# Down projections of a two-layer decoder trunk: two kinds of weight differences and one pair of activation differences take a later place in VectorE's order

## The chip, the cores and the metric

The kernel runs on one core of a Trainium2 chip. The metric is the device time of one execution in microseconds (us). The engines are named as in the profile: PE is TensorE, PEld its weight loads, DVE is VectorE, ACT is ScalarE, POOL is GpSimd, and SP is the engine that issues most DMAs, in the order of its queue.

## What is computed

The reference is a decoder trunk of two layers over 1024 tokens of width 1024, in float32. Each layer has a mixer (retention and RWKV heads in layer 0, sliding-window attention in layer 1), and after it a dense feed-forward block. The change touches only the last product of that block, the down projection with 2816 inputs:

```python
def swiglu(h, w_gate, w_up, w_down):
    return (jax.nn.silu(h @ w_gate) * (h @ w_up)) @ w_down
...
    h = h + swiglu(n, ffn_w_gate[layer], ffn_w_up[layer], ffn_w_down[layer])
```

## The kernel before

**Precision.** Every float32 operand of a product is split in two: a high part (a cast on ACT to fp32r) and a low part (a subtraction of the cast from the source, on POOL or DVE). A product is three matmuls, high by high, high by low, low by high: lines 1182, 1183 and 1184 of `prod`. For a weight tile `vsplit` makes the cast on ACT (line 1370) and the low part on POOL (line 1371). The split weights go through six buffers in turn (`w` and `wr`), so a cast waits until PE has finished with the weight six places earlier. For an activation tile `split` makes the cast on ACT (line 356) and the low part on POOL or DVE (line 358).

**The down projection.** `down` (line 1400) multiplies 2 by 2 blocks with seven products instead of eight, after Strassen and Winograd. The 2816 inputs come in 22 tiles of 128, that is 11 pairs p (NP = 11); tokens come in two halves of 512 (h0 and h1); outputs come in eight tiles, that is four pairs dp. `DGROUPS` cuts the pairs p into groups: (0, 4) and (4, 8) in layer 0, whose rest goes another way, and (0, 4), (4, 8) and (8, 11) in layer 1. In a group of n pairs each of the four dp has a raw weight block of four parts, a11, a12, a21 and a22, from the buffers `wd0` (a11, a12) and `wd1` (a21, a22). DVE forms from them, always at line 1397 because all go through the helper `vop`:

- S1 = a21 + a22 (a buffer `ws`), and S2 = S1 - a11 (a second buffer `ws`), both in the first round;
- the third difference, S3 = a11 - a21, written over a21 in `wd1` (called at line 1446);
- the fourth difference, S4 = a12 - S2, written over S2 in its `ws` buffer (called at line 1451), so that it must wait until ACT and POOL have read S2.

**Rounds.** A group is seven rounds on PE. In each round the four dp have an accumulator (PSUM bank) of their own, and each takes 3n matmuls of 128x128 by 128x512. The weights of the rounds are: 1 a11, 2 S2, 3 a12, 4 S3, 5 a22, 6 S1, 7 S4. The activations are tiles of the hidden product or of its sums and differences: round 1 and 3 plain tiles of half 0, round 7 plain tiles of half 1 (loaded into `hr`, then split; the SP line is 1381), and round 2, 4, 5 and 6 differences that were split earlier, written to the DRAM array `hc`, and are loaded again by `sums8` (SP, line 1376) into buffers `n8` and `ha`. Behind each accumulator DVE adds the result into h0 or h1; in round 1 ACT copies it to a buffer u0 (line 1434).

**Where the differences of the activations come from.** `form_down` (line 1313) makes four differences for a pair p: a subtraction on DVE (line 1318), a split, and a DMA to `hc` from SP (line 1325). For all pairs but the last it runs during the feed-forward loop before. For the last pair of layer 1 (p = 10) it is handed to `down` as `rest` and is traced there between rounds 4 and 5 of the first group (line 1460). For that pair the low part of the split is on DVE, and the two tiles that hold a split serve in turn, so the third one waits for the first DMA. Its results are first needed in the last group.

**Order of the work.** The kernel is traced in program order, and a scheduler then orders each engine's instructions, by when it takes their inputs to be ready. `behind` adds an ordering edge between two instructions of one engine without a wait on a semaphore; `keep` pins an instruction behind all that was traced on its engine before. The loads and stores of `down` on SP are kept in this way, in program order: on SP the four stores of pair 10 (line 1325) stand ahead of the four loads of round 6 (line 1376, tiles `ha`), these ahead of the raw tiles of round 7 (line 1381), and these ahead of the next group's weights and tiles.

In the order before, DVE takes S3 of a dp right behind that dp's S2 where it is free, and S4 wherever it is ready. It runs the four subtractions of pair 10 (line 1318) ahead of the first S1 of layer 1's first group, and their low parts (line 358) in round 4.

Of the kernel before, what the change touches and what calls it, by code (L numbers as in the profile page):

```python
# [13 lines left out]
ALU = mybir.AluOpType  # L14
# [9 lines left out]
NP = FT // 2  # L24
# [180 lines left out]
class Kern:  # L205
# [456 lines left out]
    def pair(self, u, hf, p):  # L662
# [123 lines left out]
        for w in range(2):  # L786
# [4 lines left out]
            mean = self.t(mp, [P, 32], "vm", 2)[:, :8].rearrange("p (a b) -> p a b", b=2)  # L791
            V.tensor_reduce(out=mean, in_=ps, axis=AX.X, op=ALU.add, negate=True)

# [33 lines left out]
    def unit(self, u, hf, pairs):  # L827
# [10 lines left out]
        for q in range(2):  # L838
            nc.sync.dma_start(DT[64 * q : 64 * q + 64], dn)
        X = self.t(mp, [P, 16, 32], "X", 1)  # L840
        Xf = X.rearrange("p a b -> p (a b)")
        G.memset(Xf, 0.0)
# [4 lines left out]
        for j in range(31):  # L847
            n, m = j // 2 + 1, 31 - j
            tv = tmp[:, : n * m].rearrange("p (a b) -> p a b", b=m)
            V.tensor_tensor(  # L850
                out=tv, in0=X[:, 0:n, j : j + 1].to_broadcast([P, n, m]),
                in1=DT[:, j : j + 1, j + 1 : 32].to_broadcast([P, n, m]), op=ALU.mult,
            )
            V.tensor_tensor(out=X[:, 0:n, j + 1 : 32], in0=X[:, 0:n, j + 1 : 32], in1=tv, op=ALU.add)
            if j % 2:
                yield (), 1.9
        for q in range(2):
            nc.sync.dma_start(dg.rearrange("u (i q) t -> q u i t", q=2)[q], X[64 * q : 64 * q + 64])
        if u:
# [453 lines left out]
    def form_down(self, L, p, x, ts):  # L1313

        nc = self.nc

        def put(i, o, a, b):
            nc.vector.tensor_tensor(out=o, in0=a, in1=b, op=ALU.subtract)
            t = ts[i in (2, 3)]
            self.split(o, t[:, 0, :], t[:, 1, :], p < NP - 1)  # L1320
            d = (self.hc[L][p, i - 1], t.bitcast(F32))
            if p == NP - 2 and i > 2:
                self.owed.append(d)
            else:
                (nc.gpsimd if p == NP - 2 else nc.sync).dma_start(*d)
            return o

        tmp = lambda: self.t(self.pp, [P, HT], "nq", 4)
        yield
        t1 = put(1, x["11"], x["12"], x["11"])  # L1330
        yield
        t2 = put(2, tmp(), x["22"], t1)
        yield
        put(4, tmp(), x["21"], t2)
        yield
        put(3, tmp(), x["22"], x["12"])
        yield
# [62 lines left out]
    def down(self, L, fp, fz, rest, X, first):  # L1400


        op, S = self.vop, self.nc.scalar
        h0, h1 = (self.kt(self.h[hf]) for hf in range(2))
        dps = range(KT // 2)
        j, ends = len(X), []

        def place():
            nonlocal j
            i, j = j % (12 if L else 14), j + 1  # L1410
            if i >= 8 if L else i < 6:
                return self.t(fp, [P, 2, HT], "ha", 4 if L else 6, F32R)
            return self.t(self.pp, [P, 2, HT], "n8", 8, F32R)

        def plain(hf, f):
            return self.plain8(L, hf, f, place(), self.t(fp, [P, HT], "hr", 4))

        for gi, g in enumerate(DGROUPS[L]):
            n, ps = g[1] - g[0], range(*g)
            ta, tb = ("fffy", "mmrc")[:: 1 - 2 * (gi % 2)]  # L1420
            s1, u0, a1 = [], [], []
            W = [self.wdown(L, 0, g, fp, "wd0", 5)]
            X = X or [plain(0, 2 * p) for p in ps]
            W += [self.wdown(L, 2 * i, g, fp, "wd0", 5) for i in (1, 2, 3)]
            for i in dps:
                W[i] += self.wdown(L, 2 * i + 1, g, fp, "wd1", 6 - L)
            A = [self.pst(t, [P, HT]) for t in ta]
            first += [self.vsplit(W[dp][0]) for dp in dps[len(first) :]]
            cast = self.last_cast
            for dp in dps:  # L1430
                a11, a12, a21, a22 = W[dp]
                self.prod(A[dp], first[dp], X, True, False)
                u0.append(self.t(fz, [P, HT], "u0", 4))
                self.behind(S.copy(u0[dp], A[dp]), cast)
                s1.append(op(self.wsum(fp, n, 4, 8), a21, a22))
                if ends:
                    self.behind(self.last_vop, ends[dp])
                a1.append(a11)
                W[dp][0] = op(self.wsum(fp, n, 4, 8), s1[dp], a11, ALU.subtract)
            X = [self.sums8(L, p, 2, place()) for p in ps]  # L1440
            B = [self.pst(t, [P, HT]) for t in tb]
            for dp in dps:
                self.prod(B[dp], self.vsplit(W[dp][0]), X, True, False)
                y = op(self.t(fz, [P, HT], "y", 2), B[dp], u0[dp])
                op(h1(2 * dp), h1(2 * dp), y)
                op(W[dp][2], a1[dp], W[dp][2], ALU.subtract)
            X = [plain(0, 2 * p + 1) for p in ps]
            for dp in dps:
                self.prod(A[dp], self.vsplit(W[dp][1]), X, False, True)
                op(h0(2 * dp), h0(2 * dp), A[dp])  # L1450
                op(W[dp][0], W[dp][1], W[dp][0], ALU.subtract)
            X = [self.sums8(L, p, 3, place()) for p in ps]
            for dp in dps:
                self.prod(B[dp], self.vsplit(W[dp][2]), X, False, False)
                y = op(self.t(fz, [P, HT], "y", 2), B[dp], u0[dp])
                op(h1(2 * dp + 1), h1(2 * dp + 1), y)
            X = [self.sums8(L, p, 4, place()) for p in ps]
            while self.owed:
                self.keep(self.nc.sync.dma_start(*self.owed.pop(0)))
            for _ in rest:  # L1460
                pass
            for dp in dps:
                self.prod(B[dp], self.vsplit(W[dp][3]), X, False, True)
                op(u0[dp], B[dp], u0[dp])
                op(h0(2 * dp + 1), h0(2 * dp + 1), u0[dp])
            X = [self.sums8(L, p, 1, place()) for p in ps]
            X6 = [plain(1, 2 * p + 1) for p in ps]
            if g[1] == NP:
                yield
            A = [self.pst(t, [P, HT]) for t in ta]  # L1470
            for dp in dps:
                self.prod(A[dp], self.vsplit(s1[dp]), X, True, False)
                op(h1(2 * dp + 1), h1(2 * dp + 1), A[dp])
            ends, first = [], []
            for dp in dps:
                self.prod(A[dp], self.vsplit(W[dp][0]), X6, False, True)
                op(h1(2 * dp), h1(2 * dp), A[dp])
                ends.append(self.last_vop)
            X = ()
        yield  # L1480
# [402 lines left out]
```

## Time and profile before

| what | value |
|---|---|
| median of 3 runs | 2357.8 us (2355.4 to 2360.68) |
| the profiled execution's own time | 2357.52 us |
| its span in the profile | 2355.7 us |
| mean granted clock of PE | 0.993 of full speed |
| first group of layer 0, round 2 begins | 1156.50 us after the start of the span |
| first group of layer 1, round 2 begins | 2137.63 us after the start of the span |

Times in the rows are microseconds from the start of the span, and a second number is the duration, which is given in nanoseconds only where the profile says so. A row of the timeline has start, duration, engine, line, operation, output<-input, shapes and how many instructions were merged, and in square brackets how long the engine had been idle and what ended that. A row of the waits has the waiting engine, tile and line, behind the arrow the releaser, then the sum in us, how many waits, and the longest. Matmuls overlap, so what one costs is read from the distance of the starts. The span leaves out about 1.8 us of the execution's own time.

### The profile page before, as it was taken

The page shows a single profiled execution, that of the slowest core. Times are in us where ns is not written, and L with a number is a line of the kernel's source. Part 1 is how long each engine was busy: PE and PEld are TensorE (multiplying, and loading weights), DVE is VectorE, ACT ScalarE, POOL GpSimd, SP SyncE. Part 2 cuts the span into 40 slices and gives each one's busy share as a digit, 9 for nine tenths or more (in the row PEclk, how much of TensorE's full clock was granted, in tenths as well). Part 3 has the DMA queues.
Part 4 walks back from the last instruction along what each step waited for, and adds up shares of the span by engine and source line. Part 5 has one row for each costly group of instructions (what it writes and reads, how often), then busy time and mean ns, then how long its engine had stood idle before and what let it go on. Part 6 is the DMA issues. An engine that isn't in the chain of part 4 may idle for free.

```text
span 2355.7 us, 35610 instructions
## 1 busy us (share of the span) xinstructions
PE 2306.3 (98%) x13092; PEld 1826.9 (78%) x13092; DVE 1650.4 (70%) x2628; ACT 1051.2 (45%) x1944; POOL 953.7 (40%) x748
## 2 busy tenths in 40 slices
PE   8999999999999999999999999999999999999998
PEld 6777677777777888888888877677788888887886
DVE  6876865765657448887676568667647788888766
ACT  5354433323556333333333556556635333333335
POOL 3123221201342057777577300002201677776776
PEclk9999999999999999999999999999999999999999
DMA  7655543433445646554574321131236466656663
GB/s 275 211 192 199 172 152 130 127 123 117 143 165 171 209 161 212 213 204 172 181 267 146 128 79 57 67 132 71 95 117 216 172 219 216 216 201 245 257 213 114
DMA packets 168317, 398.02 MB, mean 169 GB/s; under 512 B 42960, under 2 KB 45648, under 8 KB 168144
## 3 DMA queue, kind: packets, MB, share of 16 engines
q1 hardware_dynamic: 165024, 390.24, 47.6%
q10 hardware_dynamic: 2832, 4.45, 0.5%
q8 instruction: 104, 1.70, 0.3%
q0 software_dynamic: 288, 1.05, 0.1%
q14 instruction: 69, 0.57, 0.1%
HBM read 273.39 MB, written 116.92 MB: 166 GB/s over the span
## 4 chain that ended last, share of the span: by engine, by line
PE 75%; DVE 10%; DMA 5%; issue 4%; ACT 3%; POOL 1%; SPq 1%; DVEq 0%; ACTq 0%; POOLq 0%
PE ps_m L1182 7%; PE ps_m L1184 7%; PE ps_m L1183 7%; PE ps_f L240 6%; PE ps_f L352 5%; PE ps_f L351 5%; PE ps_f L350 5%; PE ps_m L240 4%; PE ps_f L1182 4%; PE ps_f L1184 4%; PE ps_f L1183 4%; PE ps_r L1182 2%; PE ps_r L1184 2%; PE ps_r L1183 2%; PE ps_c L1182 2%
## 5 line engine op out<-in xcount | busy, mean ns | idle before, releaser
L240 PE MATMUL ps_f<-n,w 128*128 128x512 f32 x1440 | 386.5, 416 | 10.8 <-ACT w L335 6.3
L240 PEld LDWEIGHTS ps_f<-n,w 128*128 128x128 f32 x1440 | 269.4, 193 | 95.4 <-issue 24.1
L335 ACT CAST w<-wr 128x512 fp32r<-128x512 f32 x244 | 148.0, 612 | 184.2 <-PE ps_f L352 71.3
L336 POOL TENSOR_TENSOR w<-wr,w 128x512 fp32r<-128x512 f32 x68 | 91.5, 1354 | 280.5 <-ACT w L335 223.4
L336 DVE TENSOR_TENSOR w<-wr,w 128x512 fp32r<-128x512 f32 (+1 forms) x176 | 123.4, 704 | 73.7 <-ACT w L335 73.5
L336 POOL TENSOR_TENSOR w<-wq,w 128x512 fp32r<-128x512 f32 x92 | 131.2, 1438 | 39.3 <-ACT w L335 36.9
L350 PE MATMUL ps_f<-n,w 128*128 128x512 f32 x356 | 141.4, 397 | 0.7 <-ACT n L1629 0.5
L351 PE MATMUL ps_f<-n,w 128*128 128x512 f32 x356 | 141.7, 398 | 0.0
L352 PE MATMUL ps_f<-n,w 128*128 128x512 f32 x356 | 140.9, 396 | 0.6 <-POOL w L336 0.6
L336 POOL TENSOR_TENSOR wx<-wr,wx 128x512 fp32r<-128x512 f32 x8 | 10.5, 1318 | 303.1 <-ACT wx L335 302.9
L1191 DVE TENSOR_TENSOR nq<-ps_m,u 128x512 f32<-128x512 f32 x88 | 58.9, 684 | 99.3 <-PE ps_m L1184 99.1
L1182 PE MATMUL ps_f<-n,w 128*128 128x512 f32 x298 | 117.4, 395 | 1.6 <-ACT u L1342 1.6
L1182 PE MATMUL ps_m<-n,w 128*128 128x512 f32 x300 | 117.6, 392 | 0.0
L1184 PE MATMUL ps_m<-n,w 128*128 128x512 f32 x300 | 116.9, 390 | 0.0
L1183 PE MATMUL ps_m<-n,w 128*128 128x512 f32 x300 | 116.8, 389 | 0.0
L1183 PE MATMUL ps_f<-n,w 128*128 128x512 f32 x298 | 116.1, 390 | 0.0
L1184 PE MATMUL ps_f<-n,w 128*128 128x512 f32 x298 | 115.9, 391 | 0.0
L1182 PE MATMUL ps_m<-cb,w 128*128 128x512 f32 x240 | 93.6, 390 | 1.3 <-DVE nq L1191 1.3
L1184 PE MATMUL ps_m<-cb,w 128*128 128x512 f32 x240 | 93.4, 389 | 0.0
L1183 PE MATMUL ps_m<-cb,w 128*128 128x512 f32 x240 | 93.4, 389 | 0.0
L358 POOL TENSOR_TENSOR n<-nq,n 128x512 fp32r<-128x512 f32 x54 | 91.6, 1708 | 4.0 <-ACT n L356 4.0
L1371 POOL TENSOR_TENSOR w<-wd,w 128x512 fp32r<-128x512 f32 (+1 forms) x51 | 72.3, 1427 | 36.9 <-ACT w L1370 36.9
(532 smaller groups left out, 6447.1 us busy)
## 6 DMA issues: line engine op xcount, KB each, us to landing
hc<-n SPq DMA_DIRECT2D x74, 512.0 KB, 2.7
wsp<-w SPq DMA_DIRECT2D x54, 512.0 KB, 3.7
w<-wsp SPq DMA_DIRECT2D x54, 512.0 KB, 3.4
wq<-in_w_gate SPq DMA_DIRECT2D x44, 512.0 KB, 4.2
u<-u SPq DMA_DIRECT2D x88, 256.0 KB, 3.0
n<-hc SPq DMA_DIRECT2D x43, 512.0 KB, 5.9
wr<-in_w_in SPq DMA_DIRECT2D x34, 512.0 KB, 5.1
hid<-n SPq DMA_DIRECT2D x66, 256.0 KB, 2.0
```

Source lines behind the costliest of these rows:

```text
L240: self.nc.tensor.matmul(out, lhsT, rhs, **kw)
L335: nc.scalar.copy(hi[:, :n], raw[:, c])
L336: self.lo.tensor_tensor(out=lo[:, :n], in0=raw[:, c], in1=hi.bitcast(F32)[:, :n], op=ALU.subtract)
L350: nc.tensor.matmul(ps, hi, rh, start=k == 0, stop=False)
L351: nc.tensor.matmul(ps, hi, rl, start=False, stop=False)
L352: nc.tensor.matmul(ps, lo, rh, start=False, stop=k == n - 1)
L358: e.tensor_tensor(out=lo, in0=src, in1=hi.bitcast(F32), op=ALU.subtract)
L1182: mm(ps, hi, xh, start=first and k == 0, stop=False, skip_group_check=True)
L1183: mm(ps, hi, xl, start=False, stop=False, skip_group_check=True)
L1184: mm(ps, lo, xh, start=False, stop=last and k == len(w) - 1, skip_group_check=True)
L1191: self.last_add = V.tensor_tensor(out=o, in0=x, in1=y, op=ALU.add)
L1371: nc.gpsimd.tensor_tensor(out=lo, in0=v, in1=hi.bitcast(F32), op=ALU.subtract)
```

## The change

S3 and S4 of every dp get an ordering edge behind the last S2 of their group (`s2`). The subtractions of pair 10 in layer 1 are kept behind all DVE work that was traced before them, which ends with the additions of round 4 of the first group. No instruction is added or removed, and SP's order is the same in both kernels.

```diff
@@ form_down
         def put(i, o, a, b):
-            nc.vector.tensor_tensor(out=o, in0=a, in1=b, op=ALU.subtract)
+            j = nc.vector.tensor_tensor(out=o, in0=a, in1=b, op=ALU.subtract)
+            if p == NP - 1:
+                self.keep(j)
             t = ts[i in (2, 3)]
             self.split(o, t[:, 0, :], t[:, 1, :], p < NP - 1)
...
@@ down
                 W[dp][0] = op(self.wsum(fp, n, 4, 8), s1[dp], a11, ALU.subtract)
+            s2 = self.last_vop
             X = [self.sums8(L, p, 2, place()) for p in ps]
             B = [self.pst(t, [P, HT]) for t in tb]
             for dp in dps:
...
                 op(W[dp][2], a1[dp], W[dp][2], ALU.subtract)
+                self.behind(self.last_vop, s2)
             X = [plain(0, 2 * p + 1) for p in ps]
             for dp in dps:
                 self.prod(A[dp], self.vsplit(W[dp][1]), X, False, True)
                 op(h0(2 * dp), h0(2 * dp), A[dp])
                 op(W[dp][0], W[dp][1], W[dp][0], ALU.subtract)
+                self.behind(self.last_vop, s2)
```

In the instruction order of the two builds, DVE's row for the first group of either layer becomes S1 and S2 of dp 0 to 3, then the four S3, then the four S4. In the later groups the additions of the round before stand between the S1 and S2 as they did. In layer 1 the order behind round 4 becomes: first subtraction of pair 10; then for each dp of round 5 the result taken from the accumulator, the low part of one difference, the subtraction of the next one, and the addition into h0; the fourth low part stands behind the fourth result. ACT's casts of these four differences go from rounds 4 and 5 to stand between the casts for S1 and S4 (rounds 6 and 7). PE's order changes in round 2 (the fourth dp's first matmuls move up to the first activation tile), slightly in round 3, and in round 6 of layer 1's first group: there the four dp take the first `ha` tile, then the four dp the second one, where before one dp took all four tiles.

## The prediction

> **What bounds the kernel now.** I read the page's busy times first, then PE's waits in the two stretches that the change touches, then the timelines there. From the page:
>
> ```profile
> PE 2306.3 (98%) x13092; PEld 1826.9 (78%) x13092; DVE 1650.4 (70%) x2628; ACT 1051.2 (45%) x1944; POOL 953.7 (40%) x748
> ```
>
> PE is busy in 98% of the span. So a later or earlier DVE instruction is worth nothing unless PE stands still for it. PE's waits from 1130 to 1290 us (layer 0's down projection) and, below the dots, from 2080 to 2360 us (layer 1's):
>
> ```profile
> PE ps_r L1182 <- ACT wr L1370: 1.4, 1, 1.4
> ...
> PE ps_r L1182 <- ACT wr L1370: 1.3, 1, 1.3
> PE ps_m L1184 <- POOL wr L1371: 0.9, 1, 0.9
> ```
>
> By the timelines below all three are in round 2 of a layer's first group: PE wants the split S2 of the second and third dp. The later groups have no wait at all, so there the change has nothing to win. PE's timeline in layer 1's round 2, and the first matmul of its round 3:
>
> ```profile
> 2137.63 0.39 PE L1182 MATMUL ps_m<-n,w 128*128 128x512 f32 x1
> ...
> 2138.78 0.50 PE L1182 MATMUL ps_m<-n,wr 128*128 128x512 f32 x1 [0.31 <-ACT wr L1370]
> ...
> 2140.46 0.51 PE L1184 MATMUL ps_m<-n,wr 128*128 128x512 f32 x1 [0.94 <-POOL wr L1371]
> 2142.26 0.50 PE L1182 MATMUL ps_r<-n,wr 128*128 128x512 f32 x1 [1.30 <-ACT wr L1370]
> ...
> 2143.54 0.63 PE L1182 MATMUL ps_m<-n,wr 128*128 128x512 f32 x1
> ...
> 2146.10 0.63 PE L1184 MATMUL ps_r<-n,wr 128*128 128x512 f32 x1
> ...
> 2153.53 0.84 PE L1182 MATMUL ps_f<-ha,w 128*128 128x512 f32 x3
> ```
>
> The round lasts 2153.53 - 2137.63 = 15.9 us. What it would last without waits is shown by round 6 of the same group, with the same 48 matmuls, from its first matmul to that of round 7:
>
> ```profile
> 2186.18 0.39 PE L1182 MATMUL ps_f<-ha,w 128*128 128x512 f32 x1
> ...
> 2197.05 0.39 PE L1182 MATMUL ps_f<-n,wr 128*128 128x512 f32 x1
> ```
>
> That is 10.87 us, 0.2265 a matmul. Round 2 of layer 1 loses **5.0 us**. Of that 1.6 us is no wait: from 2143.54 to 2146.10 six steps take 0.43 us each, and the windows view has the clock (busy time, count, granted clock, DMA share, GB/s):
>
> ```profile
> 1160.00:1164.00 4.00, 4.00 (x19) 1.00 0.00 0
> 2142.40:2147.00 4.60, 4.60 (x14) 0.63 0.68 276
> ```
>
> At 0.63 of full speed 4.6 us hold 0.37 x 4.6 = 1.7 us of lost clock; I take 1.6, eight matmuls that last 0.2 us longer. Layer 0's round 2:
>
> ```profile
> 1156.50 0.39 PE L1182 MATMUL ps_m<-ha,w 128*128 128x512 f32 x1
> ...
> 1157.75 0.51 PE L1184 MATMUL ps_m<-ha,wr 128*128 128x512 f32 x1
> 1159.60 0.50 PE L1182 MATMUL ps_r<-ha,wr 128*128 128x512 f32 x1 [1.35 <-ACT wr L1370]
> ```
>
> The seventh matmul begins at 1159.60 instead of 1156.50 + 6 x 0.2265 = 1157.86, so 1.7 us are lost; the clock behind it is 1.00 (the first row of the windows).
>
> **The change, part 1: S2 ahead of S3 and S4, layer 0.** DVE, then ACT, then POOL:
>
> ```profile
> 1156.48 1.76 DVE L1397 TENSOR_TENSOR ws<-wd,ws 128x512 f32<-128x512 f32 x1 [3.45 <-POOL w L1371]
> 1158.16 0.68 DVE L1397 TENSOR_TENSOR ws<-ws,wd 128x512 f32<-128x512 f32 x1
> ...
> 1156.70 0.59 ACT L1434 COPY u<-ps_y 128x512 f32<-128x512 f32 x1 [1.09 <-PE ps_y L1184]
> 1158.93 0.62 ACT L1370 CAST wr<-ws 128x512 fp32r<-128x512 f32 x1 [1.65 <-DVE ws L1397]
> ...
> 1159.63 1.57 POOL L1371 TENSOR_TENSOR wr<-ws,wr 128x512 fp32r<-128x512 f32 x1 [1.94 <-ACT wr L1370]
> ```
>
> The first row is S4 of dp 0. It waits 3.45 us for POOL to have read the S2 that it overwrites, and the S2 of dp 2 stands behind it. In the new order all S2 are done some 3 us before 1156.5, and the cast of dp 2 only waits for its place on ACT, behind the copy: 1156.70 + 0.59 + 0.62 = 1157.9, due at 1157.86. Its low part then takes POOL 1.57 us as in the last row, to 1159.5 (1.81 us is the longest in the rows below). The matmul that needs it is the eleventh in the new PE order, due at 1156.50 + 10 x 0.2265 = 1158.8. So 0.7 us of waiting remain, and more if POOL is late with dp 1 too, because DVE's S3 now run beside it. At most the whole 1.7 us are won; at least 0.3, if POOL is one 1.1 us turn later (1.78 less 0.68, below). I take **-1.0**.
>
> **Part 2: the same in layer 1, with pair 10 out of the way.** DVE, then ACT, then the last three weight loads on SP and their median time to landing:
>
> ```profile
> 2129.09 1.66 DVE L1318 TENSOR_TENSOR n<-n,n 128x512 f32<-128x512 f32 x1
> ...
> 2133.77 0.68 DVE L1397 TENSOR_TENSOR ws<-wd 128x512 f32<-128x512 f32 x1
> ...
> 2139.20 1.75 DVE L1397 TENSOR_TENSOR ws<-wd,ws 128x512 f32<-128x512 f32 x1
> ...
> 2144.38 0.68 DVE L1397 TENSOR_TENSOR ws<-ws,wd 128x512 f32<-128x512 f32 x1
> ...
> 2138.63 0.58 ACT L1434 COPY u<-ps_y 128x512 f32<-128x512 f32 x1
> ...
> 2127.39 1.28 SPq L1389 DMA_DIRECT2D wd<-in_w_down  x3
> wd<-in_w_down SPq DMA_DIRECT2D x3, 512.0 KB, 4.4
> ```
>
> Pair 10's four subtractions hold DVE from 2129.09 to 2133.77; the last S2 comes at 2144.38. Without them and without S3 and S4 in between, DVE is free at 2129.1. The last three blocks land by 2127.4 + 1.3 + 4.4 = 2133.1, and the two subtractions of the last one end by 2134.5, 2136 if POOL slows two of them to 1.75. ACT copies the fourth accumulator as soon as round 1 ends (2137.6 to 2138.3) and casts the fourth S2 by 2139.0. In the new PE order the tenth matmul needs it: 2137.63 + 9 x 0.2265 = 2139.7. No wait is left, and without waits I expect no half rate: **-5.0**. Behind the last S2 (2136) stand eight S3 and S4 and two low parts for round 3, which now begins at 2148.5 and takes the first of the two six matmuls on, at 2149.9. Ten such instructions take 6 us at the 0.60 us pitch of part 3, and each of POOL's splits that they meet adds 1.1 us: POOL has six in that time (two S2, two a12, two tiles), 12.6 us for the 13.9 there are. I count nothing, and up to 3 us in the range, since it is close.
>
> In the later groups the S2 come earlier and S3 and S4 later, but those are cast two and five rounds on; with 10.9 us a round I count 0.
>
> **Part 3: pair 10 behind round 4.** SP, then the time to landing of the first load of `ha`:
>
> ```profile
> 2174.57 0.32 SPq L1325 DMA_DIRECT2D hc<-n  x1
> 2174.98 2.14 SPq L1376 DMA_DIRECT2D ha<-hc  x4
> ...
> ha<-hc SPq DMA_DIRECT2D x1, 512.0 KB, 5.4
> ```
>
> This is the price. The first row is pair 10's fourth store, the next are the four loads for round 6, queued behind it. The first lands at 2174.98 + 5.4 = 2180.4, and PE wants it at 2186.18 (above): 5.8 us of slack. All times of this part are on the old clock; parts 1 and 2 move everything here by the same amount. The fourth store now waits for the fourth low part, which on DVE stands behind the fourth accumulator of round 5. DVE around the end of round 4 and in round 5, then POOL:
>
> ```profile
> 2173.87 0.68 DVE L358 TENSOR_TENSOR n<-nq,n 128x512 fp32r<-128x512 f32 x1
> 2174.47 1.78 DVE L1397 TENSOR_TENSOR h<-h,y 128x512 f32<-128x512 f32 x1
> 2176.17 0.68 DVE L1397 TENSOR_TENSOR y<-ps_c,u 128x512 f32<-128x512 f32 x1
> ...
> 2178.22 0.69 DVE L1397 TENSOR_TENSOR u<-ps_m,u 128x512 f32<-128x512 f32 x1
> ...
> 2186.70 0.68 DVE L1397 TENSOR_TENSOR u<-ps_c,u 128x512 f32<-128x512 f32 x1
> ...
> 2178.97 1.81 POOL L1371 TENSOR_TENSOR w<-ws,w 128x512 fp32r<-128x512 f32 x1 [1.41 <-ACT w L1370]
> ```
>
> Starts follow each other at 0.60 us, or at 1.70 where a DVE row lasts 1.78 (2174.47 to 2176.17), which happens when both engines work out of SBUF. From 2178.22 on each dp has four DVE instructions (result, low part, next subtraction, addition). Lower bound, paced by PE: the fourth result at 2186.70, the fourth low part done 1.3 us later, 2188.0. Upper: each dp also meets one POOL split (the 1.81 row): 3 x 0.60 + 1.70 = 3.5 us a dp, the fourth result at 2178.22 + 10.5 = 2188.7, the low part done at 2190.0. I take the upper, since POOL has one such split for every dp of this round. The store goes out at 2190.0, the first load 0.4 later, and lands 5.4 later: 2195.8. PE wants it at 2186.2: a new wait of **+9.6**. The bounds are 6.6 (2188.0, landing in 4.4 like the weights) and 13 (two POOL splits met per dp, 1.1 us each).
>
> After so long a wait I add one stretch at half rate, **+1.6**, as after the 2.5 us of waits in round 2; between 0 and twice that.
>
> Queued behind `ha` are the raw tiles of round 7. ACT's row for their casts before:
>
> ```profile
> 2184.83 2.51 ACT L356 CAST n<-hr 128x512 fp32r<-128x512 f32 x4 [0.50 <-DMA hr<-hid]
> ```
>
> They end at 2187.3. With the loads 15.4 us later (2190.4 for 2174.98) it is 2202.7, while round 7 goes from 2197.05 to 2208.3; 5.6 us are left for two low parts each on POOL and DVE. I count 0, and up to 3 us for this and for the next group's weights behind it.
>
> **Sum**: -1.0 - 5.0 + 9.6 + 1.6 = **+5.2 us**. The profiled execution took 2357.5 us (span 2355.7), which gives 2362.7; its time is 0.3 below the median of the runs, 2357.8, and on that the same sum is **2363.0**.
>
> **Rivals.**
> 1. DVE keeps pace with PE in round 5: the store at 2188.0, a wait of 7.4 us, +3.0 in all: 2360.8; with a landing in 4.4 us and no half rate it is 6.6 - 6.0, 2358.4. For it: four instructions at 0.60 are 2.4 us, less than the 2.72 us that PE takes for a dp. Against it: one met split makes it 3.5.
> 2. The transfers for round 6 stay hidden, and only the gain is left: 2357.8 - 6.0 = 2351.8, faster. That decides itself at one point: the fourth store must be out by 2180.4 on the old clock, 5.8 us of slack behind 2174.57. It speaks against it that PE ends the fourth accumulator of round 5, behind which the low part stands, only at 2186.2.
> 3. The late loads also stop round 7 or the next group: 3 us more, 2366, up to 2369 with a second stretch at half rate.
> 4. The half rate in round 2 is no consequence of the waits, and comes back at 1.6 us: 2364.6. For it: layer 0's 1.35 us wait was followed by a full clock. Against it: the half rate begins 1.3 us behind the last wait.
>
> The Trainium skill (TensorE: Matmul & The Clock Gate, Part 1) has the half rate come after an idle window of about 3.4 us. By that rule the waits in round 2, none over 1.3 us in the trace, would not cause it, and the sum would be rival 4's; the trace has it right behind three such waits within 4 us, so I give the rule less.
>
> **How the numbers follow.** Forecast 0.50, rival 1 0.26, rival 2 0.06, rival 3 0.11, rival 4 0.07. 0.2% (4.7 us) is about what a measurement of this kernel can tell from no change. The forecast itself is 0.5 us beyond that, with some 1.5 us either way, so I split it 0.31 slower and 0.19 same; rivals 3 and 4 are slower, rival 1 same with a little slower. That makes 0.50 slower, 0.44 same, 0.06 faster. The range leaves out rival 2 and the far end of rival 3: 2357.0 to 2368.5.
>
> **What would show it.** Round 2 of layer 1's first group in about 10.9 us at full clock, and of layer 0's in about 11.5. In layer 1 the four stores of line 1325 spread over round 5, and a PE wait of 7 to 11 us on the DMA of `ha` ahead of round 6, with a granted clock near 0.6 behind it. Wrong would be: no such wait, an `ha` load issued before the fourth store, or a wait in round 3 or 7.

## The result, and the profile after

The changed kernel takes 2370.9 us (median of six runs, 2369.3 to 2374.6) where the kernel before takes 2358.2 (median of six as well, 2355.4 to 2360.7): a ratio of 1.0059, interval 1.0046 to 1.0071. It is slower, by 12.7 us. The profiled execution took 2369.4 us with a span of 2367.6, 11.9 us more than before.

Line numbers behind line 1320 are two higher than before, or a little more (1397 is now 1399). PE's busy time is nearly what it was, so the new time is PE standing still or running slowly:

```profile
PE 2308.3 (97%) x13092; PEld 1828.4 (77%) x13092; DVE 1662.1 (70%) x2628; ACT 1051.9 (44%) x1944; POOL 953.2 (40%) x748
```

PE's waits from 2080 to 2370 us (layer 1's down projection): the waits of before's round 2 are gone, and two others are there.

```profile
PE ps_f L1182 <- DMA ha<-hc: 10.1, 1, 10.1
PE ps_f L1183 <- DVE ha L358: 2.2, 1, 2.2
```

PE's timeline has the first matmuls of rounds 2, 3, 4 and 6 and of the next group in layer 1, and the matmuls around the two waits:

```profile
2137.69 0.39 PE L1182 MATMUL ps_m<-n,w 128*128 128x512 f32 x1
...
2149.05 0.62 PE L1182 MATMUL ps_f<-ha,w 128*128 128x512 f32 x2
...
2149.95 0.39 PE L1182 MATMUL ps_f<-ha,w 128*128 128x512 f32 x1
2152.49 0.50 PE L1183 MATMUL ps_f<-ha,w 128*128 128x512 f32 x1 [2.15 <-DVE ha L358]
...
2153.20 0.63 PE L1182 MATMUL ps_f<-ha,w 128*128 128x512 f32 x1
...
2163.96 0.39 PE L1182 MATMUL ps_m<-n,wr 128*128 128x512 f32 x1
...
2195.94 0.77 PE L1182 MATMUL ps_f<-ha,w 128*128 128x512 f32 x1 [10.06 <-DMA ha<-hc]
...
2220.01 0.39 PE L1182 MATMUL ps_m<-n,w 128*128 128x512 f32 x1
```

From start to start, round 2 takes 11.36 us (15.90 before), round 3 14.91 (10.88), rounds 4 and 5 with the wait behind them 31.98 (21.77), rounds 6 and 7 24.07 (21.75). That is -4.5, +4.0, +10.2 and +2.3 us; with -0.2 in layer 0 it makes +11.8, close to the 11.9 us by which the spans differ. The stretches that the change does not touch also differ between the two traces, by up to 1.6 us, but here they cancel. The windows view (busy time, count, granted clock, DMA share, GB/s) shows the half rate behind both waits:

```profile
2152.50:2156.20 3.70, 3.70 (x10) 0.55 1.04 414
...
2195.90:2200.70 4.80, 4.76 (x11) 0.50 1.04 412
```

**Round 3.** PE waits there for the low part of a tile, which DVE forms. DVE's timeline from the first S1 on:

```profile
2128.86 1.77 DVE L1399 TENSOR_TENSOR ws<-wd 128x512 f32<-128x512 f32 x1
...
2137.70 1.67 DVE L1399 TENSOR_TENSOR ws<-ws,wd 128x512 f32<-128x512 f32 x1
2139.29 4.69 DVE L1399 TENSOR_TENSOR wd<-wd,wd 128x512 f32<-128x512 f32 x4
2143.90 6.87 DVE L1399 TENSOR_TENSOR ws<-wd,ws 128x512 f32<-128x512 f32 x4
2150.70 3.42 DVE L358 TENSOR_TENSOR ha<-hr,ha 128x512 fp32r<-128x512 f32 x2
```

The rows are the first S1, the last S2, the four S3, the four S4 and the two low parts. DVE is never idle. The last S2 ends at 2139.3, and the first low part is done only at about 2152.4, while PE is ready for it at 2150.2. POOL beside it:

```profile
2140.10 1.63 POOL L1373 TENSOR_TENSOR w<-ws,w 128x512 fp32r<-128x512 f32 x1 [1.28 <-ACT w L1372]
2141.69 3.43 POOL L1373 TENSOR_TENSOR w<-wd,w 128x512 fp32r<-128x512 f32 x2
2145.09 3.43 POOL L358 TENSOR_TENSOR ha<-hr,ha 128x512 fp32r<-128x512 f32 x2
2148.49 1.74 POOL L1373 TENSOR_TENSOR w<-wd,w 128x512 fp32r<-128x512 f32 x1
2150.19 3.39 POOL L1373 TENSOR_TENSOR wr<-wd,wr 128x512 fp32r<-128x512 f32 x2
```

DVE's ten instructions from 2139.29 to 2154.12 take 14.8 us. POOL runs eight splits in that time. With 0.60 us for each DVE instruction and 1.1 us more for each split of POOL that it meets, that is 10 x 0.60 + 8 x 1.1 = 14.8.

**Round 6.** SP's timeline; the first row is pair 10's four stores, the second the four loads of `ha` queued behind them. Then DVE's row of the fourth low part, which the fourth store waits for:

```profile
2179.55 10.80 SPq L1327 DMA_DIRECT2D hc<-n  x4
2190.45 2.16 SPq L1378 DMA_DIRECT2D ha<-hc  x4
```

```profile
2189.33 0.67 DVE L358 TENSOR_TENSOR n<-nq,n 128x512 fp32r<-128x512 f32 x1
```

The low part ends at 2190.0, the load goes out at 2190.45, and PE starts at 2195.94, 5.5 us later. This is the prediction's chain, step by step.

**Layer 0.** PE's waits from 1130 to 1290 us, then POOL and DVE in round 2:

```profile
PE ps_m L1184 <- POOL wr L1373: 0.7, 1, 0.7
PE ps_r L1184 <- POOL wr L1373: 0.3, 1, 0.3
```

```profile
1156.73 1.69 POOL L1373 TENSOR_TENSOR w<-ws,w 128x512 fp32r<-128x512 f32 x1 [7.13 <-ACT w L1372]
1158.38 3.43 POOL L1373 TENSOR_TENSOR wr<-ws,wr 128x512 fp32r<-128x512 f32 x2
```

```profile
1155.38 3.58 DVE L1399 TENSOR_TENSOR wd<-wd,wd 128x512 f32<-128x512 f32 x4
1158.89 6.87 DVE L1399 TENSOR_TENSOR ws<-wd,ws 128x512 f32<-128x512 f32 x4
```

The wait has moved from ACT's cast to POOL's low parts, and round 2 is only 0.2 us shorter. POOL's low parts come 1.7 us apart, because DVE's S3 and S4 now run beside them.

### The profile page after: what moved, and what is told of

It reads as the page before. It is cut to its first block, busy times and chain, and to the rows that moved or that the text cites. A ratio compares the mean times of both kernels' runs of the same rounds, so it can differ in the third digit from the quotient of the medians.

```text
span 2367.6 us, 35618 instructions
## 1 busy us (share of the span) xinstructions
PE 2308.3 (97%) x13092; PEld 1828.4 (77%) x13092; DVE 1662.1 (70%) x2628; ACT 1051.9 (44%) x1944; POOL 953.2 (40%) x748
## 4 chain that ended last, share of the span: by engine, by line
PE 77%; DVE 8%; ACT 4%; issue 3%; DMA 3%; POOL 1%; SPq 0%; DVEq 0%; ACTq 0%; POOLq 0%
PE ps_f L240 7%; PE ps_m L1182 7%; PE ps_m L1184 7%; PE ps_m L1183 7%; PE ps_f L352 5%; PE ps_f L351 5%; PE ps_f L350 5%; PE ps_m L240 5%; PE ps_f L1182 4%; PE ps_f L1184 4%; PE ps_f L1183 4%; PE ps_r L1184 2%; PE ps_r L1182 2%; PE ps_r L1183 2%; PE ps_c L1184 2%
```

## The experiments

The theory after the result: the three losses are separate, each with its own cause. Round 3 is lost because S3 and S4 now stand on DVE ahead of the low parts of round 3's tiles, and POOL's splits slow them; round 6 because the `ha` loads stand behind the fourth store of pair 10 on SP; the rest is half rate behind these waits. The rival: it is one loss, DVE late as a whole, which a mending of one place would only move on.

Each row of this table is one trace: us from the first matmul of a round to that of the next, in layer 0 (L0) and layer 1 (L1), then the median time and its ratio to the kernel before on the same chip, whose median was 2357.2 to 2358.8 beside the other kernels.

| kernel | L0 R2 | L1 R2 | R3 | R4, R5, wait | R6, R7 | median | ratio (95%) |
|---|---|---|---|---|---|---|---|
| before | 12.76 | 15.90 | 10.88 | 21.77 | 21.75 | 2358.2 | |
| after | 12.56 | 11.36 | 14.91 | 31.98 | 24.07 | 2370.9 | 1.0059 (1.0046 to 1.0071) |
| e1_edges | 12.55 | 15.57 | 10.96 | 21.76 | 21.76 | 2360.8 | 1.0018 (1.0004 to 1.0033) |
| e2_keep | 12.77 | 11.54 | 10.88 | 31.17 | 23.50 | 2368.4 | 1.0044 (1.0028 to 1.0060) |
| e3_pool | 12.54 | 11.36 | 14.98 | 21.76 | 23.78 | 2362.7 | 1.0016 (1.0005 to 1.0027) |
| e4_low | 12.11 | 11.23 | 10.88 | 32.30 | 23.41 | 2363.5 | 1.0022 (1.0012 to 1.0032) |
| e6_queue | 12.56 | 11.43 | 13.32 | 21.76 | 21.76 | 2359.4 | 1.0009 (0.9997 to 1.0021) |
| e7_keepq | 12.79 | 11.59 | 10.88 | 21.76 | 21.76 | 2352.3 | 0.9985 (0.9975 to 0.9996) |
| e8_all | 12.10 | 11.36 | 10.88 | 21.76 | 21.76 | 2354.8 | 0.9988 (0.9976 to 1.0001) |
| e9_queue_only | 12.78 | 15.72 | 10.88 | 21.76 | 21.76 | 2361.8 | 1.0011 (1.0000 to 1.0023) |
| e10_dvelow | 12.55 | 11.40 | 10.88 | 32.11 | 23.18 | 2366.7 | 1.0031 (1.0014 to 1.0049) |
| e11_again | 12.55 | 11.28 | 16.22 | 32.16 | 23.75 | 2374.9 (one run) | |

The medians carry some us that are no round's: round 1 of layer 1's first group starts anywhere from 2124.3 to 2134.3 us in these traces, and round 2 of layer 0's first group, ahead of which no edit acts, already from 1153.7 to 1163.3. So the rounds decide below, and the times only say how far they agree.

### The two halves of the change: e1_edges and e2_keep

e1 drops the `keep` of pair 10; e2 drops the two edges.

```diff
 e1_edges, in form_down:
-            j = nc.vector.tensor_tensor(out=o, in0=a, in1=b, op=ALU.subtract)
-            if p == NP - 1:
-                self.keep(j)
+            nc.vector.tensor_tensor(out=o, in0=a, in1=b, op=ALU.subtract)
 e2_keep, in down, behind S3 and behind S4:
-                self.behind(self.last_vop, s2)
```

> Only the edges that hold S3 and S4 behind the last S2; pair 10 runs ahead of S1 as in the kernel before. Theory (the fourth store in SP's queue delays round 6, and ten DVE instructions ahead of two low parts delay round 3): no wait on the DMA of ha, so the 12.5 us of round 6 in layer 1 (10.2 waited, 2.3 half rate) are gone. Pair 10 holds DVE to 2133.8 again, so the fourth S2 comes near 2143, due at 2139.7: round 2 lasts about 14.5 us (15.9 before, 11.4 after), and round 3 still waits 1 to 3 us for the low parts. 2359 to 2362 us. Rival (the late S3 and S4 are themselves the cost, through the rounds that use them): near 2370.

> Only pair 10 is kept behind round 4; S3 and S4 stand among the S2 as in the kernel before. Theory: the wait of about 10 us on the DMA of ha and the half rate behind it stay (12.5 us), round 2 of layer 1 gains about 3.5 us because pair 10 is gone, and round 3 has no wait, since S4 no longer stand in a row ahead of the low parts: about 2367 us. Rival (the two parts only hurt together, since the S4 push pair 10 back): round 6 without a wait, below 2358.

The edges alone win 0.3 us in layer 1 and 0.2 in layer 0. Round 2 took 15.57 us, not 14.5, and the expected wait in round 3 was not there. PE's waits in e1:

```profile
PE ps_r L1184 <- POOL wr L1371: 1.1, 1, 1.1
PE ps_r L1182 <- ACT wr L1370: 0.7, 1, 0.7
PE ps_m L1184 <- POOL wr L1371: 0.4, 1, 0.4
```

They sum to 2.2 us, where before had 2.5, and the half rate behind them stays. S2 is still late, because pair 10's subtractions stand ahead of it. The median, 2360.8, lies in the expected range all the same, but not for the expected reason: the rounds are 0.4 us shorter than before's, and the median is 2.0 us longer.

The `keep` alone does what the whole change does in layer 1, but for round 3: round 2 goes to 11.54 us (-4.4 of the -4.5), the wait ahead of round 6 and its half rate come, and round 3 has no loss. So the gain in round 2 is pair 10's, and the loss in round 3 comes only with the edges and the `keep` together.

### The wait ahead of round 6: e3_pool, e6_queue, e9_queue_only

e3 issues pair 10's stores from POOL. e6 keeps them on SP and puts the loads of `ha` and of round 7's raw tiles ahead of them. e9 is the kernel before with e6's edit alone.

```diff
 e3_pool, in form_down:
-            (nc.gpsimd if p == NP - 2 else nc.sync).dma_start(*d)
+            (nc.gpsimd if p >= NP - 2 else nc.sync).dma_start(*d)
 e6_queue and e9_queue_only, in down:
             X = [self.sums8(L, p, 4, place()) for p in ps]
...
+            X5 = [self.sums8(L, p, 1, place()) for p in ps]
+            raw6 = [self.t(fp, [P, HT], "hr", 4) for p in ps]
+            for p, raw in zip(ps, raw6):
+                self.keep(self.nc.sync.dma_start(raw, self.hid[2 * L + 1][2 * p + 1]))
             for _ in rest:
                 pass
...
```

> The changed kernel, but pair 10's four stores are issued by POOL instead of SP, so that nothing on SP stands ahead of the loads of ha; DVE keeps pair 10 behind round 4. Theory (the place in SP's queue is the cause): the loads go out near 2169 to 2175, round 6 begins without a wait, round 3 still loses 4.0 us: 2370.9 - 12.5 = 2358.4, up to 2.6 us more for four issues on POOL. Rival (the stores' transfers slow the loads down on the DMA engines): the wait at round 6 stays above 3 us, 2362 or more.

> The changed kernel, with SP's order alone changed: in each group the four loads of ha for round 6 and the four raw tiles of round 7 are issued ahead of pair 10's four stores. If the 10.1 us wait ahead of round 6 and the half rate behind it come from the loads being queued behind the fourth store (theory), both go: round 6 of layer 1's first group follows 21.8 us after the start of round 4, and rounds 6 and 7 take about 21.8 us; the 4.0 us lost in round 3 stay, since DVE's order up to there is the same. Time 2370.9 - 10.2 - 2.3 = 2358.4. Rival A: the four stores, now behind the loads, hold up the next group's weights or the buffers of the difference tiles, and the loss turns up in round 7 or the next group: 2360 or more. Rival B: the wait has another cause (the transfer itself is slow beside the stores): a wait on the DMA of ha of 3 us or more stays.

> The kernel before with SP's order alone changed (loads of ha and of round 7's raw tiles ahead of pair 10's stores). No wait in before goes back to that order, so no round changes by more than 0.3 us: 2358.2, within 0.2%. If it is faster by itself, part of what the two other versions win is not theirs.

In both e3 and e6 the 10 us wait and the half rate behind it are gone. So the loads were late because of the queue, not because of the transfer. In e6 rounds 4 to 7 take 43.5 us as before. Its round 3 lost 2.4 us, not the expected 4.0 (the half rate, below), and a small loss turned up in the next group, where its rival A has one, but by another way (under "Both mended"). SP's timeline of e6 shows the loads some 20 us ahead of the stores:

```profile
2160.54 2.36 SPq L1378 DMA_DIRECT2D ha<-hc  x4
...
2180.34 10.81 SPq L1327 DMA_DIRECT2D hc<-n  x4
```

e3 pays 2.0 us in rounds 6 and 7 in another way. One of PE's waits, then DVE and POOL:

```profile
PE ps_f L1182 <- DVE h L1399: 1.8, 1, 1.8
```

```profile
2184.14 6.92 DVE L1399 TENSOR_TENSOR h<-h,u 128x512 f32<-128x512 f32 x1
```

```profile
2183.62 0.57 POOL L1327 DMA_DIRECT2D hc<-n  x1
2184.22 1.31 POOL L1373 TENSOR_TENSOR wr<-ws,wr 128x512 fp32r<-128x512 f32 x1
2185.48 2.53 POOL L358 TENSOR_TENSOR n<-hr,n 128x512 fp32r<-128x512 f32 x2
2187.97 2.53 POOL L1373 TENSOR_TENSOR w<-ws,w 128x512 fp32r<-128x512 f32 x2
```

One addition on DVE lasts 6.92 us instead of 0.68. It starts with the first of five splits that POOL runs without a pause, 1.26 us apart from 2184.22 to 2190.50, and ends 0.6 us behind the last. e3's median, 2362.7, is above the expected 2358.4 to 2361.0 and where its rival has it; but the rival's sign, a wait above 3 us ahead of round 6, is not there. e9 has the rounds of before, so the queue's order by itself wins nothing there (its time is 0.1% above before's, which its rounds do not show).

### Round 3: e4_low, e10_dvelow, e11_again

e4 puts S4 of a layer's first group behind DVE's low parts of round 3's tiles. e10 leaves the order and takes four splits from POOL: in a layer's first group the low parts of a12 are formed by DVE. e11 is the changed kernel once more.

```diff
 e4_low, in split and in down:
-        e.tensor_tensor(out=lo, in0=src, in1=hi.bitcast(F32), op=ALU.subtract)
+        i = e.tensor_tensor(out=lo, in0=src, in1=hi.bitcast(F32), op=ALU.subtract)
+        if not pool_lo:
+            self.last_lo = i
...
             X = [plain(0, 2 * p + 1) for p in ps]
+            lo = self.last_lo
...
-                self.behind(self.last_vop, s2)
+                self.behind(self.last_vop, s2 if gi else lo)
 e10_dvelow, in vsplit and in down:
-    def vsplit(self, v):
+    def vsplit(self, v, e=None):
...
-        nc.gpsimd.tensor_tensor(out=lo, in0=v, in1=hi.bitcast(F32), op=ALU.subtract)
+        (e or nc.gpsimd).tensor_tensor(out=lo, in0=v, in1=hi.bitcast(F32), op=ALU.subtract)
...
-                self.prod(A[dp], self.vsplit(W[dp][1]), X, False, True)
+                self.prod(A[dp], self.vsplit(W[dp][1], None if gi else self.nc.vector), X, False, True)
```

> The changed kernel, but in a layer's first group the four S4 stand behind the two low parts that DVE makes for round 3. Theory (the row of eight differences ahead of the low parts is what round 3 waits for): the first low part near 2144 instead of 2150.7, no wait and no half rate in round 3: 2370.9 - 4.0 = 2366.9, with round 6 as in the changed kernel. Rival (POOL, which shares SBUF with DVE here, is what is late in round 3): the wait moves to a POOL split and 2 us or more stay, 2369 or more.

> The changed kernel, but in a layer's first group the low parts of round 3's weights (a12, four instructions) are formed by DVE instead of POOL. Two of them stand ahead of the first low part of round 3's tiles on DVE. Theory (DVE is late in round 3 because each POOL split that it meets costs it 1.1 us): from the start of S3 at 2139.3 DVE has ten instructions at 0.60 and meets three splits instead of eight, 9.3 us, so that the low part starts at 2148.6 instead of 2150.7 and the 2.15 us wait in round 3 of layer 1 shrinks to under 0.5: round 3 in 10.9 to 11.4 us for 14.9, and 2370.9 - 3.6 = 2367.3. The 10 us wait ahead of round 6 stays. Rival (it is the number of DVE instructions ahead, whatever POOL does): two more at the 1.4 us mean of the S3 and S4 there make the wait 2.15 + 2.8 = 5.0 us, round 3 in 17 us or more, 2373.

> The changed kernel once more, one look, for the half rate in round 3 of layer 1: behind the same wait of 2.15 us it was there in the changed kernel and in the version with stores from POOL (1.6 us lost), and not in the version with the loads ahead of the stores. If the wait decides, it is there again (round 3 in 14.9 us); if it is chance or something of the moment, it may be absent (13.3 us). The wait ahead of round 6 is 10 us and the half rate behind it there in either case.

e4: round 3 is back at 10.88 us, and nothing else moves by more than 0.7. So it is S4 ahead of the low parts. (Its time, 2363.5, is 3.4 below the expectation: the rounds add 6.9 us to before, the medians 4.7.)

e10 tells why S4 takes so long. DVE, from S3 on, and POOL:

```profile
2141.10 4.69 DVE L1399 TENSOR_TENSOR wd<-wd,wd 128x512 f32<-128x512 f32 x4
2145.72 2.98 DVE L1399 TENSOR_TENSOR ws<-wd,ws 128x512 f32<-128x512 f32 x3
2148.61 1.28 DVE L1373 TENSOR_TENSOR w<-wd,w 128x512 fp32r<-128x512 f32 x2
2149.82 0.68 DVE L1399 TENSOR_TENSOR ws<-wd,ws 128x512 f32<-128x512 f32 x1
2150.42 1.28 DVE L358 TENSOR_TENSOR ha<-hr,ha 128x512 fp32r<-128x512 f32 x2
```

```profile
2141.91 1.64 POOL L1373 TENSOR_TENSOR w<-ws,w 128x512 fp32r<-128x512 f32 x1 [1.28 <-ACT w L1372]
2143.51 3.44 POOL L358 TENSOR_TENSOR ha<-hr,ha 128x512 fp32r<-128x512 f32 x2
2151.14 1.72 POOL L1373 TENSOR_TENSOR wr<-wd,wr 128x512 fp32r<-128x512 f32 x1 [4.20 <-ACT wr L1372]
```

DVE has two more instructions ahead of the low part, and yet the low part starts 9.3 us after S3's start instead of 11.4: ten instructions at 0.60 and three met splits at 1.1 are 9.3. Round 3 takes 10.88 us. The rival (the number of DVE instructions) said 17 or more.

e11 shows the other side. DVE's timeline of e11:

```profile
2142.43 6.88 DVE L1399 TENSOR_TENSOR wd<-wd,wd 128x512 f32<-128x512 f32 x4
2149.23 6.84 DVE L1399 TENSOR_TENSOR ws<-wd,ws 128x512 f32<-128x512 f32 x4
2156.00 3.42 DVE L358 TENSOR_TENSOR ha<-hr,ha 128x512 fp32r<-128x512 f32 x2
```

Here all ten meet a split, 17.0 us = 10 x 0.60 + 10 x 1.1; the wait in round 3 is 3.6 us and the round 16.2. So the same kernel loses 4.0 us in round 3 in one execution and 5.3 in another. The same 2.15 us wait did not come back, so this run does not tell whether the half rate would follow it again.

### Both mended: e7_keepq and e8_all

e7 is e2 with e6's order on SP; e8 is e4 with that order.

> Only the keep of pair 10's subtractions, with no edges for S3 and S4, and with the loads of ha and of round 7's raw tiles ahead of pair 10's stores on SP. Theory: the keep alone wins 4.4 us in round 2 of layer 1 (11.5 us) and loses nothing in round 3 (10.9 us); without the store ahead of the loads nothing is lost ahead of round 6: 2358.2 - 4.4 = 2353.8. Rival: low parts of pair 10 on DVE, now in round 5 with no pause behind them, delay round 6 or 7 by 1 to 3 us (as the 1.8 us wait that the run with stores from POOL had there): 2355 to 2357.

> All of the change, with S4 of a layer's first group behind the DVE low parts of round 3's tiles, and with the loads of ha and of round 7's raw tiles ahead of pair 10's stores on SP. Theory: the three losses are separate, so all gains stay and none of the losses: layer 0 round 2 -0.6, layer 1 round 2 -4.7, round 3 as before, no wait ahead of round 6: 2358.2 - 5.3 = 2352.9, faster than both kernels. Rival: DVE has too much to do from round 3 on in layer 1 (S4 moved behind round 3's low parts, pair 10 in round 5) and a wait of 1 to 3 us on DVE appears in rounds 4 to 7: 2354 to 2356.

The three losses are gone in both: e7 is left with 4.3 us of gain in layer 1's round 2, e8 with 4.5 there and 0.7 in layer 0. No wait of PE between 2080 and 2370 us is over 0.4 us. e7 is faster than both kernels, 2352.3 us, 0.9985 of before (0.9975 to 0.9996).

One small loss is left in e8, and in e6, which the table does not show. Round 3 of layer 1's second group takes 11.71 us in e8 and 11.78 in e6; it takes 10.87 or 10.88 in the other ten traces. DVE in e8 has S3 and then S4 there:

```profile
2210.17 6.88 DVE L1401 TENSOR_TENSOR wd<-wd,wd 128x512 f32<-128x512 f32 x4
2216.98 5.17 DVE L1401 TENSOR_TENSOR ws<-wd,ws 128x512 f32<-128x512 f32 x3
```

All seven meet a split, and round 3's first low part on DVE starts behind them only at 2222.08, 0.55 us ahead of the round. It is the loss of the first group's round 3 once more: the edges hold in every group, and e4's repair, which is part of e8, only in the first. e7, which has no edges, does not have it. With these 0.8 us e8's rounds gain 4.4 us to e7's 4.3. e8's median is 2354.8, with an interval up to 1.0001; which of the two is better can't be told by these runs. The rival, one loss that only moves on, has fallen for the three losses of the first group.

## Why the prediction was wrong

Slower was right, but the time lies beyond the range: 2370.9 for 2363.0, and a range up to 2368.5. The range was narrower than the bounds of its own terms: with each at its upper end (-0.3 in layer 0, -5.0 in round 2, 3 in round 3, 13 for the wait, 3.2 of half rate, 3 behind it) the sum is 16.9 us, or 2374.7. Term by term, in layer 1 unless said otherwise, with the trace of after against that of before:

| term | predicted | measured |
|---|---|---|
| layer 0, round 2 | -1.0 | -0.2 |
| round 2 | -5.0 | -4.5 |
| low parts in round 3 | 0 (up to 3) | +4.0 |
| wait ahead of round 6 | +9.6 (6.6 to 13) | +10.2 |
| half rate in round 6 | +1.6 (0 to 3.2) | +2.3 |
| sum | +5.2 | +11.8 |

**The step that failed** is in part 2: "12.6 us for the 13.9 there are. I count nothing". Its place and its mechanism were named there, and two of its numbers were wrong. The last S2 was put at 2136, paced by the weight loads with two subtractions slowed; it ended at 2139.3, because five of the eight S1 and S2 met a split of POOL (8 x 0.60 + 5 x 1.1 = 10.3, from 2128.86). And six splits were counted beside S3, S4 and the low parts, where there were eight: one of the two S2 was already done, and POOL had gone on to the other two a12 and to the first S3. The ten instructions so end at 2154.1 for the 2148.6 of the prediction. The wait was 2.15 us, and 1.6 us of half rate came on top (round 3 takes 14.91 us for the 13.32 of e6, which has the same wait at full clock); the prediction charged half rate only to round 6, and its 3 us for the range did not hold the two together. e4 and e10 show the cause from two sides: with S4 out of the way, or with POOL's splits out of the way, the 4.0 us are gone. A step with 1.3 us of reserve on a count of 12.6, and with a second cost behind it if it fails, should not have stood at nothing.

**Layer 0** came out just under the prediction's own lower bound, 0.3: POOL's low part of dp 1 was late, slowed by the S3 and S4 that now run beside it. The two waits of 1.0 us together, and 0.7 us in the steps around them, took all but 0.2 of the gain. In e4 and e8, which hold S4 back there, the second wait is gone and the round takes 12.1 us for 12.56.

**Round 2** went as forecast: no wait over 0.2 us is left. The 0.5 us short of the forecast lies in small steps. The windows view of after has the clock in round 2:

```profile
2137.70:2149.00 11.30, 11.12 (x49) 1.00 1.03 414
```

With the waits the half rate is gone, at a full clock throughout; rival 4 has fallen.

**Part 3** was right in every step. DVE's results of round 5 came at 2178.07, 2181.76, 2185.26 and 2188.73, 3.55 us apart for the 3.5 of the upper bound, so rival 1 has fallen. (Its own sum is 0.2 us low: by its rows the wait is 2193.8 - 2186.2 = 7.6, not 7.4.) The wait is 10.06 us for 9.6: the load landed by 2195.9, 0.1 us from the forecast, and PE was ready 0.5 us earlier than before. Rival 2 fell with it. Round 7 and the next group lost nothing, as counted, so rival 3 has fallen too, although its time, 2366 to 2369, is nearer to the result than the forecast: the missing time was upstream of it. That the later groups lose nothing holds in after, where PE comes to them 12 us later; in e6 and e8, without that delay, one of their rounds loses 0.8 to 0.9 us.

**The half rate** is the one thing that the prediction could not place. In the traces of the down projections it followed every wait of 9 us or more (1.4 to 2.3 us lost), the 2.2 to 2.6 us of waits in pieces in round 2 of before, e1 and e9 (1.6 to 1.7), and the single waits of 2.2 us in after and e3 and of 3.6 in e11 (about 1.6 each). It did not follow the single waits of 1.4 us in layer 0, nor e3's 1.8. And it did not follow e6's wait, which is the same as that of after. PE and windows of e6:

```profile
2149.98 0.39 PE L1182 MATMUL ps_f<-ha,w 128*128 128x512 f32 x1
2152.51 0.50 PE L1183 MATMUL ps_f<-ha,w 128*128 128x512 f32 x1 [2.14 <-DVE ha L358]
```

```profile
2152.50:2156.20 3.70, 3.69 (x16) 1.00 1.05 415
```

The same 2.14 us, and a full clock behind it. What decides it can be read from the records of the granted clock in the traces. In each of the twelve traces all half-rate stretches begin on one grid with steps of 3.4133 us, within 4 ns, and the grid lies elsewhere in every execution. In after the whole wait falls into one step, 2149.47 to 2152.88, and the half rate begins with the next. In e6 the grid, carried on from the half-rate stretches elsewhere in that trace, has a point at 2150.95, inside the wait, so no step holds more than 1.56 us of it.

In the stretches from 1130 to 1300 us and from 2130 to 2300 us of the twelve traces the half rate followed every step in which PE stood for 1.68 us or more, in one wait or in pieces (the two lowest are round 2 of before and of e9), and none with 1.60 us or less (the highest is e3's 1.8 us wait, of which 1.60 us fall into one step). Other stages, with matmuls of other shapes, do not keep to these two figures. So a wait near 2.2 us costs 1.6 us more or nothing, by where it falls on the grid, and 1.6 of the 4.0 us of round 3 are chance in this sense. The Trainium skill (TensorE: Matmul & The Clock Gate, Part 1) calls the activity window of about 3.4 us free-running, so that the same kernel can differ from run to run; that fits these traces. Its rule of one idle window of that length does not: the half rate came here behind single waits of 2.15 us.

## What to carry to other kernels

Where two engines work out of the same memory, count the neighbour's instructions over the whole stretch, by its own row in the timeline, and not only those that belong to the step: here n instructions on DVE beside m splits on POOL took 0.60 n + 1.1 m us in round 3 of after, e10 and e11. Before an instruction is moved behind another stage, follow its result to the DMA that waits for it, and look at what stands behind that DMA in its queue: the move was worth 4.4 us and cost over 10, and the same move with the loads put ahead of the stores (e7) made a kernel 0.15% faster than before. A step that is close goes into the sum with a price, the half rate behind it included.

## What was not expected of the hardware

In the stretches shown DVE and POOL took turns, one instruction each: 1.70 us a pair, 0.60 of DVE and 1.1 of POOL. In e3, after POOL had issued a DMA between its splits, the turns stopped once, and one addition of DVE stood for 6.92 us while POOL ran five splits at 1.26; why is not shown. The Trainium skill (SBUF — State Buffer, Who interferes with whom) says that a VectorE instruction with two inputs in SBUF contends with a GpSimd instruction that reads SBUF, and calls it an exclusive lock. The trace agrees with that for the 1.1 us, but in e3 DVE was passed over by four more instructions.
